# Linear attention with ReLU features: K and V of two groups loaded as one transfer

## The chip, the cores and the metric

The kernel runs on one NeuronCore of one Trainium2 chip. The metric is the device time of one execution in microseconds (us); the time given for a kernel is the median of its runs.

## The reference

Q, K and V have the shape 8 x 12 x 512 x 64 in float32, so there are 96 heads of 512 rows by 64 columns.

```python
Q_feat = np.maximum(0, Q)
K_feat = np.maximum(0, K)
KV = np.einsum('bhkd,bhkv->bhdv', K_feat, V)
K_sum = np.sum(K_feat, axis=2)
numerator = np.einsum('bhqd,bhdv->bhqv', Q_feat, KV)
denominator = np.einsum('bhqd,bhd->bhq', Q_feat, K_sum)
return numerator / (denominator[:, :, :, None] + 1e-10)
```

For each head a 64 x 64 matrix KV and a vector K_sum of 64 are made from K and V; each row of Q is then multiplied by them and divided. There is no softmax, so K and V of a head must be complete before any of its output can be made.

## The kernel before

The 96 heads are worked in 12 octets of 8 heads (numbered 0 to 11), and an octet's K and V in 2 groups of 4 heads. Octet o holds the groups 2o and 2o + 1. A group's K is a tile `k_sb` of 128 partitions; a partition holds 16 rows of one head, which lie in HBM as one run of 16 x 64 x 4 bytes = 4 KB. V is the same in `v_sb`. Q of an octet is one tile `q_sb`, 128 partitions with 32 rows each, 8 KB in HBM. Output of an octet leaves from `o_sb`, 128 partitions with 8 KB each.

The loads are issued from POOL (GpSimd, `nc.gpsimd.dma_start`) and change float32 to bfloat16 on their way, so the 4 KB of a row arrive as 2 KB. The K and V of octet 0 are the exception: they come as float32 over the SP and ACT queues (L109, L110, `k_first` and `v_first`). For each later octet, `load_octet` issues five transfers in this order: K and V of the first group, K and V of the second group (`load_kv`, L97 and L99), then Q (`load_q`, L103). Octets 1 to 5 are issued ahead of all work. Octet o + 6 is issued in `store` (L279), just behind the store of octet o (L289), which POOL issues too. POOL issues in program order, so a store whose `o_sb` is not ready holds up the loads behind it. The stores of the last two octets go over SP (L284, L287) and the last one is cut into two halves.

The transfers of POOL share eight completion semaphores in turn: a transfer is issued only when the one eight before it has landed. The tile framework puts that wait there. It doesn't stand in the code, and it shows in the profile as POOL waiting for a `k_sb`, `v_sb`, `q_sb` or `out_dram` transfer.

The order of the compute work is written out by hand (`manual_schedule`), one instruction stream per engine. In iteration o of the main loop (L326) and up to o = 8:

- `kvs(o)`: TensorE multiplies K by V for both groups of octet o (L189) into `ps_kv`, and ACT moves the result to `kvd` (L199);
- `prep(2o+2)`, `prep_v(2o+2)`: VectorE (DVE) and ACT make masked copies of K and V of the next octet's first group (L175, L177, L182);
- `backs(o-1)`: TensorE transposes octet o - 1 back (L267), DVE divides into `o_sb` (L273), and the store is issued;
- `denom(o)`, `out_t(o)`: the denominators (L249, L252, L257, L261) and the numerators (L240, L242);
- `prep(2o+3)`, `prep_v(2o+3)`: the second group (L175, L177, L184);
- `qt(o+1)`: Q of the next octet is transposed (L210) and passed through the ReLU (L218).

The later iterations and the part behind the loop do the same in another order, so that the last stores come early. The buffers for `k_sb` and `v_sb` hold 12 groups each.

Of the kernel before, what the change touches and what calls it, by code (L numbers as in the profile page):

```python
# [10 lines left out]
def kernel(  # L11
# [7 lines left out]
    nc = tc.nc  # L19
    B, H, S, D = Q.shape  # L20
    assert D == 64
    P = 128
# [4 lines left out]
    R = S * 4 // P  # L27
# [4 lines left out]
    NO = NG // 2  # L32
    assert NO * 8 == NH and R == 16 and RQ == 32
    DELAY = 5

    fp32 = mybir.dt.float32
    bf16 = mybir.dt.bfloat16
# [3 lines left out]
    def pool(name, bufs, **kw):  # L41
        return ctx.enter_context(tc.tile_pool(name=name, bufs=bufs, **kw))

    consts = pool("consts", 1)
    qin = pool("qin", 7)
    kin = pool("kin", 12)
    vin = pool("vin", 12)
    kfp = pool("kfp", 4)
    rcp = pool("rcp", 2)
    outp = pool("outp", DELAY + 2)  # L50
# [6 lines left out]
    def view(X, f):  # L57
        return X.rearrange("b h s d -> (b h s d)").rearrange("(n p f) -> n p f", p=P, f=f)

    Qr, Kr, Vr, Or = view(Q, RQ * D), view(K, R * D), view(V, R * D), view(out, RQ * D)  # L60
# [31 lines left out]

    q_sb, k_sb, v_sb = {}, {}, {}

    def load_kv(g):
        k_sb[g] = kin.tile([P, R, D], bf16, name="k_sb")
        nc.gpsimd.dma_start(out=k_sb[g].rearrange("p r d -> p (r d)"), in_=Kr[g], single_packet=True)  # L97
        v_sb[g] = vin.tile([P, R, D], bf16, name="v_sb")
        nc.gpsimd.dma_start(out=v_sb[g].rearrange("p r d -> p (r d)"), in_=Vr[g], single_packet=True)  # L99

    def load_q(o):
        q_sb[o] = qin.tile([P, U, 2 * D], bf16, name="q_sb")
        nc.gpsimd.dma_start(out=q_sb[o].rearrange("p u f -> p (u f)"), in_=Qr[o], single_packet=True)  # L103
# [8 lines left out]
    make_identity(nc, ident)  # L112

    def load_octet(o):
        load_kv(2 * o)
        load_kv(2 * o + 1)
        load_q(o)

    for o in range(1, DELAY + 1):
        load_octet(o)  # L120
# [158 lines left out]
    def store(o, o_sb):  # L279
        Ov = Or[o].rearrange("p (r d) -> p r d", d=D)  # L280
        if o == NO - 1:
            for j in range(2):
                rs = slice(RQ // 2 * j, RQ // 2 * (j + 1))
                nc.sync.dma_start(out=Ov[:, rs], in_=o_sb[:, rs])  # L284
            return
        if o >= NO - 2:
            nc.sync.dma_start(out=Ov, in_=o_sb)  # L287
            return
        nc.gpsimd.dma_start(out=Ov, in_=o_sb, single_packet=True)  # L289
        if o + DELAY + 1 < NO:  # L290
            load_octet(o + DELAY + 1)
# [51 lines left out]
    o = NO - 2  # L343
    g = 2 * NO - 2
# [52 lines left out]
```

## Time and profile before

| What | Value |
|---|---|
| median of 3 runs | 127.1 us (126.67 to 127.52) |
| the profiled execution | 126.42 us |
| its span, first to last instruction | 124.7 us |
| instructions | 2642 |
| TensorE, VectorE, ScalarE, GpSimd busy | 69%, 67%, 65%, 31% of the span |
| mean busy share of the DMA engines | 90% or more in 38 of 40 slices |
| HBM read and written | 37.75 MB and 12.58 MB |
| transfers issued by POOL | 66: 22 of K, 22 of V, 12 of Q, 10 stores |
| transfers issued by SP and ACT | 5 |

Busy shares are means over the span. The span is what the profile shows of an execution; 1.7 us of the execution lie around it. A "DMA packet" in the profile is one row of a transfer, or one of the 16 packets of 4 bytes (one for each DMA engine) that end a transfer. The megabytes under the queues count what arrives, so a row of K counts 2 KB there though 4 KB of HBM were read.

### The profile page before, as it was taken

To read this page: it belongs to the slowest core of one execution; us is meant where nothing else is said; L and a number is where in the kernel's file an instruction comes from. 1 tells how busy PE (TensorE), PEld (TensorE's weight loads), DVE (VectorE), ACT (ScalarE), POOL (GpSimd) and SP (SyncE) were. 2 spreads that over 40 slices of the span, in tenths; PEclk is the share of its full clock that TensorE was granted. 3 is DMA by queue.
4 is the path that set the end of the run, shared out by engine and by line. 5 is a ranking of instruction groups with operands and counts; after the bars stand their busy time and mean duration, and the time that the engine had idled before them with its cause. 6 is when DMAs were issued, how large, how long until landed. Compare 5 with 4: busy or idle time off the path is not lost.

```text
span 124.7 us, 2642 instructions
## 1 busy us (share of the span) xinstructions
PE 86.4 (69%) x1067; PEld 77.5 (62%) x1067; DVE 83.1 (67%) x192; ACT 80.8 (65%) x112; POOL 38.1 (31%) x72
## 2 busy tenths in 40 slices
PE   0005794688989979897883799793696598697700
PEld 0005573687878879784872798692685497695500
DVE  2719804979899797979569346929739608979430
ACT  0008958969899898989886428976489266537100
POOL 6902624405245241233253144243333220100000
PEclk9999999999999999999999559999999859999997
DMA  3999999999999999999999999999999999999992
GB/s 95 397 310 205 216 205 210 215 206 215 206 214 210 210 216 358 229 216 333 257 213 291 299 210 256 335 210 234 354 220 217 352 233 218 323 426 415 429 410 121
DMA packets 10236, 32.67 MB, mean 262 GB/s; under 512 B 1136, under 2 KB 1136, under 8 KB 8560
## 3 DMA queue, kind: packets, MB, share of 16 engines
q0 software_dynamic: 9504, 28.32, 94.9%
q1 hardware_dynamic: 576, 3.15, 6.3%
q10 hardware_dynamic: 144, 1.05, 2.1%
q8 instruction: 8, 0.13, 0.4%
q14 instruction: 4, 0.03, 0.1%
HBM read 37.75 MB, written 12.58 MB: 404 GB/s over the span
## 4 chain that ended last, share of the span: by engine, by line
DVE 34%; DMA 27%; PE 24%; ACT 6%; issue 4%; DVEq 1%; ACTq 0%
DVE o_sb L273 15%; DMA q_sb<-in_Q_dram 11%; DMA v_sb<-in_V_dram 9%; PE ps_kv L189 8%; PE ps_bk L267 7%; DMA v_first<-in_V_dram 7%; DVE kf L175 5%; PE ps_kv L165 5%; DVE vo_all L177 3%; PE ps_qt L210 3%; DVE vo_all L184 3%; DVE den L257 2%; DVE rec L261 2%; DVE own L252 2%; ACT vo_all L158 2%
## 5 line engine op out<-in xcount | busy, mean ns | idle before, releaser
L273 DVE TENSOR_TENSOR o_sb<-ps_bk,rec 128x1024 f32<-128x1024 f32 x24 | 28.3, 1218 | 14.6 <-PE ps_bk L267 14.6
L189 PE MATMUL ps_kv<-vo_all,kf 128*128 128x132 bf16 x352 | 26.3, 234 | 6.6 <-DVE vo_all L184 6.1
L189 PEld LDWEIGHTS <-kf 128*128 128x128 bf16 x352 | 23.8, 104 | 7.9 <-issue 4.2
L242 ACT COPY ot_sb<-ps_ot 128x1024 f32<-128x1024 f32 x24 | 24.1, 1012 | 5.3 <-PE ps_ot L240 4.4
L199 ACT CAST kvd<-ps_kv 64x260 bf16<-64x260 f32 (+1 forms) x46 | 16.5, 360 | 15.2 <-PE ps_kv L189 14.1
L210 PE MATMUL ps_qt<-ident,q_sb 128*128 128x128 bf16 x192 | 15.2, 242 | 13.6 <-DMA q_sb<-in_Q_dram 13.6
L218 ACT ACTIVATE qt<-ps_qt 128x1024 bf16<-128x1024 bf16 x23 | 22.4, 1024 | 2.3 <-PE ps_qt L210 2.2
L267 PE MATMUL ps_bk<-ident,ot_sb 128*128 128x128 f32 x192 | 23.4, 276 | 0.4 <-ACT ot_sb L242 0.4
L175 DVE TENSOR_SCALAR kf<-k_sb,mask 128x1024 bf16<-128x1024 bf16 x44 | 18.3, 458 | 7.6 <-DMA k_sb<-in_K_dram 7.5
L210 PEld LDWEIGHTS <-q_sb 128*128 128x128 bf16 x192 | 13.6, 110 | 14.5 <-DMA q_sb<-in_Q_dram 14.4
L267 PEld LDWEIGHTS ps_bk<-ident,ot_sb 128*128 128x128 f32 x192 | 21.3, 144 | 0.7 <-ACT ot_sb L242 0.7
L97 POOL DMA_DIRECT2D k_sb<-in_K_dram x22 | 13.2, 602 | 25.3 <-DMA q_sb<-in_Q_dram 21.1
L240 PE MATMUL ps_ot<-qt,kvd 128*128 128x256 bf16 x96 | 14.0, 271 | 8.0 <-DVE o_sb L273 7.2
L99 POOL DMA_DIRECT2D v_sb<-in_V_dram x22 | 12.1, 551 | 20.3 <-ACT qt L218 6.4
L240 PEld LDWEIGHTS <-kvd 128*128 128x128 bf16 x96 | 9.0, 97 | 10.9 <-issue 9.0
L182 ACT ACTIVATE vo_all<-v_sb,mask 128x1024 bf16<-128x1024 bf16 x10 | 11.5, 1153 | 0.6 <-DMA v_sb<-in_V_dram 0.4
L177 DVE TENSOR_SCALAR vo_all<-v_sb,mask 128x1024 bf16<-128x1024 bf16 x22 | 10.6, 482 | 1.1 <-DMA v_sb<-in_V_dram 1.1
L289 POOL DMA_DIRECT2D out_dram<-o_sb x10 | 5.4, 544 | 13.7 <-DVE o_sb L273 4.8
L103 POOL DMA_DIRECT2D q_sb<-in_Q_dram x12 | 6.8, 570 | 8.9 <-DMA k_sb<-in_K_dram 2.7
L249 PEld LDWEIGHTS <-qt 128*128 128x128 bf16 x192 | 6.8, 96 | 3.8 <-issue 1.8
L249 PE MATMUL ps_den<-kvd,qt 128*128 128x16 bf16 x192 | 7.2, 180 | 2.3 <-ACT kvd L169 1.7
L158 ACT ACT_TABLE_LOAD x1 | 1.3, 1283 | 9.8 <-DMA v_first<-in_V_dram 9.8
(33 smaller groups left out, 50.6 us busy)
## 6 DMA issues: line engine op xcount, KB each, us to landing
out_dram<-o_sb POOLq DMA_DIRECT2D x10, 1024.0 KB, 14.3
q_sb<-in_Q_dram POOLq DMA_DIRECT2D x12, 512.0 KB, 13.1
k_sb<-in_K_dram POOLq DMA_DIRECT2D x22, 256.0 KB, 12.1
v_sb<-in_V_dram POOLq DMA_DIRECT2D x22, 256.0 KB, 12.1
v_first<-in_V_dram ACTq DMA_DIRECT2D x1, 1024.0 KB, 9.0
k_first<-in_K_dram SPq DMA_DIRECT2D x1, 1024.0 KB, 8.8
out_dram<-o_sb SPq DMA_DIRECT2D x1, 1024.0 KB, 7.0
out_dram<-o_sb SPq DMA_DIRECT2D x2, 512.0 KB, 4.2
```

Of the source, the lines that this page charges most:

```text
L97: nc.gpsimd.dma_start(out=k_sb[g].rearrange("p r d -> p (r d)"), in_=Kr[g], single_packet=True)
L175: nc.vector.tensor_scalar(kf[g][:, :, s, :], k_sb[g], scalar1=0.0, scalar2=mask[:, 0, s:s + 1], op0=Alu.max, op1=Alu.mult)
L177: nc.vector.tensor_scalar(vo[g % NB][:, :, 0, 2:D + 2], v_sb[g], scalar1=mask[:, 1, 0:1], scalar2=None, op0=Alu.mult)
L189: nc.tensor.matmul(ps_kv[:, g % 2, 0:2 * (D + 2)].rearrange("p (t d) -> p t d", t=2), kf[g][:, r, :, :].rearrange("p s d -> p (s d)"), vo[ ...
L199: copy(kvd[o % NK][64 * c:64 * c + 64, 4 * gs.start + s:4 * gs.stop:2, c * D1:c * D1 + D1].rearrange("p (g t) d -> p g t d", t=2), ps_kv[6 ...
L210: nc.tensor.transpose(ps[:, u, :], q_sb[o][:, i * (U // 2) + u, :], ident)
L218: nc.scalar.activation(to, ps, Act.Relu)
L240: nc.tensor.matmul(ps[:, i], kvd[o % NK][:, h, 1:2 * D + 1], q[:, :, h, :], start=True, stop=True, skip_group_check=True)
L242: nc.scalar.copy(ot[o][:, :, 4 * j:4 * j + 4], ps.rearrange("p h u c -> p u h c"))
L249: nc.tensor.matmul(ps[:, u], qt_sb[o % NZ][:, u, :], kvd[o % NK][:, :, 0:2 * D1:2 * D1 - 1], start=True, stop=True, skip_group_check=True)
L267: nc.tensor.transpose(ps[:, 2 * v:2 * v + 2].rearrange("p c d -> p (c d)"), ot[o][:, 8 * j + v].rearrange("p h c -> p (h c)"), ident32)
L273: nc.vector.tensor_tensor(o_sb[:, rs], ps, rec[o][:, rs].unsqueeze(2).to_broadcast([P, 16, D]), op=Alu.mult)
```

## The change

For octets 1 to 8 (`PAIRS` is 9), K of both groups is loaded by one transfer of 2 x 128 rows of 4 KB into one tile with room for two groups, and V by another. The order in the queue becomes K of both groups, V of both groups, Q. Octets 9 to 11 still load their groups one by one, in the order K, V, K, V, Q, but into the halves of such double tiles. The tiles `k_sb` and `v_sb` come from pools with 6 double buffers, which hold 12 groups as before. What the compute engines do, and in which order, is not changed.

```diff
-    kin = pool("kin", 12)
-    vin = pool("vin", 12)
+    kin = pool("kin", DELAY + 1)
+    vin = pool("vin", DELAY + 1)
...
-    def load_kv(g):
-        k_sb[g] = kin.tile([P, R, D], bf16, name="k_sb")
-        nc.gpsimd.dma_start(out=k_sb[g].rearrange("p r d -> p (r d)"), in_=Kr[g], single_packet=True)
-        v_sb[g] = vin.tile([P, R, D], bf16, name="v_sb")
-        nc.gpsimd.dma_start(out=v_sb[g].rearrange("p r d -> p (r d)"), in_=Vr[g], single_packet=True)
+    PAIRS = NO - 3
+
+    def load_kv(o, X, pool_, sb, name):
+        t = pool_.tile([P, 2, R, D], bf16, name=name)
+        for i in range(2):
+            sb[2 * o + i] = t[:, i]
+        if o < PAIRS:
+            nc.gpsimd.dma_start(out=t.rearrange("p n r d -> p n (r d)"),
+                                in_=X[2 * o:2 * o + 2].rearrange("n p f -> p n f"), single_packet=True)
+
+    def load_half(o, i, X, sb):
+        nc.gpsimd.dma_start(out=sb[2 * o + i].rearrange("p r d -> p (r d)"), in_=X[2 * o + i], single_packet=True)
...
     def load_octet(o):
-        load_kv(2 * o)
-        load_kv(2 * o + 1)
+        load_kv(o, Kr, kin, k_sb, "k_sb")
+        load_kv(o, Vr, vin, v_sb, "v_sb")
+        if o >= PAIRS:
+            for i in range(2):
+                load_half(o, i, Kr, k_sb)
+                load_half(o, i, Vr, v_sb)
         load_q(o)
```

## The prediction

> **What bounds the kernel.** I read the page's engine and DMA parts first.
>
> ```profile
> PE 86.4 (69%) x1067; PEld 77.5 (62%) x1067; DVE 83.1 (67%) x192; ACT 80.8 (65%) x112; POOL 38.1 (31%) x72
> ...
> DMA  3999999999999999999999999999999999999992
> ...
> DMA packets 10236, 32.67 MB, mean 262 GB/s; under 512 B 1136, under 2 KB 1136, under 8 KB 8560
> ...
> q0 software_dynamic: 9504, 28.32, 94.9%
> ...
> HBM read 37.75 MB, written 12.58 MB: 404 GB/s over the span
> ```
>
> No compute engine is over 69%, while the DMA engines are busy from the second slice to the last but one. The third and fourth lines give the make-up of the queue: 9504 packets in 66 transfers are 144 each, 128 rows and 16 closing packets of 4 bytes (71 transfers in all x 16 = 1136, the packets under 512 B). Each of the 16 engines thus moves 8 rows and one closing packet of every transfer.
>
> Next, POOL in the timeline, which shows how fast the queue drains, since each issue here ends a wait for the landing of the transfer issued eight before it (columns: start, duration, engine, line, operation; in brackets the idle time before).
>
> ```profile
> 29.69 0.53 POOL L103 DMA_DIRECT2D q_sb<-in_Q_dram  x1 [0.77 <-DMA v_sb<-in_V_dram]
> 30.93 0.53 POOL L97 DMA_DIRECT2D k_sb<-in_K_dram  x1 [0.71 <-DMA k_sb<-in_K_dram]
> 32.16 0.53 POOL L99 DMA_DIRECT2D v_sb<-in_V_dram  x1 [0.70 <-DMA v_sb<-in_V_dram]
> 34.62 0.53 POOL L97 DMA_DIRECT2D k_sb<-in_K_dram  x1 [1.93 <-DMA q_sb<-in_Q_dram]
> ```
>
> Two transfers of K or V, of 0.52 MB, land 1.24 and 1.23 us apart, and a Q of 1.05 MB takes 2.46 us. Twice 1.235 is 2.47, so one large transfer costs nearly what two small ones do. The trace's packet records are finer. On one engine the closing packets stand 1253 ns apart for K and V, 2458 for Q and 2464 for a store, to the nanosecond, over long stretches. Rows of K start every 154 ns. 8 x 154 = 1232, so the rest of a transfer, its closing packet, is about 21 ns; the record of that packet lasts 22 ns.
>
> Last, the chain that ended last and VectorE (DVE) around the octets where the new transfers end.
>
> ```profile
> 72.66 11.46 DMA v_sb<-in_V_dram
> ```
> ```profile
> 72.97 0.88 DVE L175 TENSOR_SCALAR kf<-k_sb,mask 128x1024 bf16<-128x1024 bf16 x2 [3.26 <-DMA k_sb<-in_K_dram]
> 74.30 0.49 DVE L177 TENSOR_SCALAR vo_all<-v_sb,mask 128x1024 bf16<-128x1024 bf16 x1 [0.45 <-DMA v_sb<-in_V_dram]
> 75.88 2.36 DVE L273 TENSOR_TENSOR o_sb<-ps_bk,rec 128x1024 f32<-128x1024 f32 x2 [1.09 <-PE ps_bk L267]
> ...
> 82.93 0.88 DVE L175 TENSOR_SCALAR kf<-k_sb,mask 128x1024 bf16<-128x1024 bf16 x2 [2.04 <-DMA k_sb<-in_K_dram]
> 84.14 0.49 DVE L177 TENSOR_SCALAR vo_all<-v_sb,mask 128x1024 bf16<-128x1024 bf16 x1 [0.33 <-DMA v_sb<-in_V_dram]
> ```
> ```profile
> 114.23 0.34 SPq L287 DMA_DIRECT2D out_dram<-o_sb  x1
> 118.36 1.46 SPq L284 DMA_DIRECT2D out_dram<-o_sb  x2
> ```
>
> The chain waits for V of group 18 (octet 9) until 84.12 and is compute from there to the last stores. But those stores don't set the end alone. The packet records show 15 to 21 packets under way at nearly every microsecond from 4 to 121. The last closing packets of the last store come from 121.8 on the first engine to 123.4 on the slowest, which has worked without a pause. The time is what the slowest DMA engine has to do. The last half-store is issued at 119.49, would need 0.83 us to start (as the first half, 118.36 to its first packet at 119.19), and the slowest engine reaches it only at 123.41 - 1.26 = 122.15: it could come 122.15 - 120.32 = 1.8 us later at no cost.
>
> **The change, part by part.**
>
> Bytes and rows stay: 16 x 16 = 256 rows per engine go into the 16 new transfers.
>
> Closing packets: 32 transfers become 16. 16 x 21 ns = 0.34 us less on every engine, the slowest too, and on the path, since that engine never pauses. The POOL rows above bound it: 2 x 1.235 - 2.46 = 0.01 us per pair, 0.16 in all; the record's own 22 ns gives 0.35. I take 0.35, and the 0.16 stays in the range. On this the Trainium skill ("DMA: Bandwidth & Descriptors", the section "Anatomy of one DMA — SWDGE (gpsimd) path") says that the write of the semaphore is a bubble of about one cycle. By that sentence the saving would be nil and the sum the time before; the 21 ns between the last row and the next transfer disagree with it here.
>
> Row cost in a double transfer: each engine now steps between two places 512 KB apart, 4 KB at each. No transfer before does that. Nearest rows: half of an 8 KB row of Q is (2458 - 21) / 16 = 152 ns; a 4 KB row of the last half-stores starts 156 ns after the one before; and a K row's record lasts 173 ns though the next starts after 154, so 173 is the price if rows no longer overlapped. Over 256 rows these ends are -0.4, +0.5 and +4.9 us. I take 154 and so 0, because read size, written size and row are those of the K rows, and keep both ends.
>
> Issue on POOL: 16 instructions fewer, at 0.55 to 0.60 us each about 9 us less. A double one could take from 0.53 (a Q issue of twice the bytes) to 2 x 0.60 = 1.2 us. Neither counts: POOL idles 0.7 to 1.9 us before each issue above, behind seven transfers still in flight. Without that cover 0.6 us x 16 = 10 us would be exposed. At the start, where eight issues follow each other from 1.26 to 6.2 us, the queue has Q of octet 0 to move until 10.4, so nothing runs dry.
>
> Eight in flight: an octet and its store are now four transfers of 1 MB instead of six. Eight of them last 8 x 2.46 = 19.7 us instead of 13.2, so stores are issued some 6 us earlier against their landing. The loads queued behind a store on POOL wait for its `o_sb`; the outputs of octets 0 to 3 are ready some octets before, and later the queue merely holds less. The order in the queue, hence each landing, stays. No cost. Pool space is the same 12 groups, whose readers finish octets earlier.
>
> Order K, K, V, V: K of the first group lands with the second, 1.25 us later, V 2 x 1.25 = 2.5 us later. Until octet 5 compute runs behind the loads: a period of 7.1 us in the chain (the `own` at 29.80, 36.89 and 43.99) against 3 x 2.46 = 7.4 us of loads, with the loads some 13 us ahead. By my reckoning V of octet 5 lands at 47.3 and is wanted at 47.4. From octet 6 the loads lead, 9.9 us an octet. Then DVE stalls with L273, L252 and the rest of the iteration queued behind its L177. Worst placed is octet 8: L177 moves from 74.30 to 76.8. Behind it come 0.48 + 2.36 + 1.2 (L252, L257, L261) + 1.6 (L175, L177, L184) to 82.4, 1.1 of TensorE at L189 and 1.6 of ACT at L199 to 85.1. In the trace of before ACT's copy L182 for group 18 ran from 84.20 to 85.35 and its next, L242, waited until 86.50. So the copy ends at 86.3 and nearly all the delay is swallowed; about 0.2 us is left, against 1.8 us of slack at the last store. No cost.
>
> Halves in octets 9 to 11: same transfers, same rows, nothing.
>
> Sum: 126.42 - 0.35 = 126.07 us for the profiled execution. The median of the runs, 127.1, is 0.7 above that execution, so the forecast is 127.1 - 0.35 = **126.8 us**. A measurement of this kernel can tell about 1% (1.3 us) from no change, so this would read as no change.
>
> **Rivals.**
>
> Dearer rows (slower). The two places 512 KB apart cost each row overlap. It decides from (1.27 + 0.35) us / 256 = 6.3 ns a row, 160 instead of 154. At 164, halfway to 173, it is 126.8 + 2.6 = 129.4; at 173, 131.7. For it: no row of before shows such stepping. Against it: K, V, Q and stores all run at the same 150 to 156 ns per 4 KB, whatever their direction and place. The Trainium skill ("DMA: Bandwidth & Descriptors", "Latency and other measured facts") reports 207 instead of 214 GB/s for rows at a pitch of 512 KiB. No run here shows it; 3.4% of 154 ns would be 5.2 ns a row, 256 x 5.2 = 1.3 us, and a time of 128.1.
>
> Late V (slower or same). If nothing swallows the 2.5 us and TensorE meets a granted clock of a half there too, as the page shows for two stretches (L189 1.80 instead of 1.11 us, L210 1.71 instead of 0.89), 1.5 us comes on top: 4.0 - 1.8 of slack = 2.2 late, 129.0. For it: DVE waits for K and V at just this place. Against it: the reckoning above, and 9.9 - 7.1 = 2.8 us free in each octet.
>
> Evener engines (faster). If the engines ended together at 122.4 instead of 121.8 to 123.4, and rows cost 152 ns: 126.8 - 1.0 - 0.4 = 125.4. For it: the spread is there. Against it: every transfer gives each engine the same share, and pairing doesn't alter that.
>
> Small ones: the double transfer is carried out as two (127.1), or the second half of a tile is made to wait for the first in octets 9 to 11. Q of octet 0 needs 4.2 us from its issue (1.26) to its first packet (5.43), so three dry spells of up to 4.2 - 1.25 us give 135. Against this, the two halves of the last store already go out separately.
>
> **How the numbers follow.** Forecast 0.51 (126.3 to 127.3 by itself), dearer rows 0.22, late V 0.12, evener engines 0.09, done as two 0.03, waiting halves 0.03. Slower by over 1%: 0.17 of dearer rows, 0.06 of late V, the 0.03, and 0.02 of the forecast's spread, 0.28. Faster by over 1%: 0.08 of evener engines and 0.02, 0.10. The rest, 0.62, within 1%. Range: 125.6, with half of the evener engines, to 129.8, past both middle prices.
>
> **What would show it.** Right: 50 transfers on the POOL queue; closing packets 2 x 1253 - 21 = 2485 ns apart for double ones; DMA busy in every slice but the ends; the end 0.35 us earlier. Wrong: rows over 160 ns apart, a dip in the DMA row at octets 9 to 11, or the last SP stores issued more than 1.8 us later.

## The result and the profile after

The changed kernel takes 126.2 us (5 runs, 125.96 to 126.35) beside 126.89 us of the kernel before (5 runs, 126.67 to 127.52): ratio 0.9933, 95% interval 0.9904 to 0.9962, so 0.5 to 1.2 us less. A second set of runs (e8 below) gave 0.9962, interval 0.9941 to 0.9984. Both lie within 1%. The forecast was 126.8 us, from a base of 127.1 us that two more runs brought to 126.89. The profiled execution went from 126.42 to 126.20 us and its span from 124.65 to 124.42. Among the runs below, only the three longest of e12 fell in a slower state, and its ratio leaves them out.

The page of the changed kernel, parts 1 to 3:

```profile
PE 84.5 (68%) x1067; PEld 75.2 (60%) x1067; DVE 83.2 (67%) x192; ACT 80.5 (65%) x112; POOL 32.4 (26%) x56
...
DMA  2999999999999999999999999999999999999992
...
DMA packets 9980, 32.67 MB, mean 263 GB/s; under 512 B 880, under 2 KB 880, under 8 KB 8304
...
q0 software_dynamic: 9248, 28.31, 94.8%
```

The small packets went from 1136 to 880, 256 = 16 x 16 fewer, and the queue has 16 x 272 + 34 x 144 = 9248 packets. The DMA engines are as busy as before, and of the others only POOL moves by more than 2 points of share, from 31% to 26%.

POOL in the timeline, with the double transfers (L102) and the time to landing from part 6:

```profile
13.65 0.85 POOL L110 DMA_DIRECT2D q_sb<-in_Q_dram  x1 [1.75 <-DMA k_sb<-in_K_dram]
16.11 0.70 POOL L102 DMA_DIRECT2D k_sb<-in_K_dram  x1 [1.61 <-DMA v_sb<-in_V_dram]
18.56 0.71 POOL L102 DMA_DIRECT2D v_sb<-in_V_dram  x1 [1.76 <-DMA q_sb<-in_Q_dram]
```
```profile
k_sb<-in_K_dram POOLq DMA_DIRECT2D x8, 512.0 KB, 19.5
...
k_sb<-in_K_dram POOLq DMA_DIRECT2D x6, 256.0 KB, 13.4
```

A double transfer lands every 2.46 us or so, and eight in flight now last 19.5 us. In the packet records the closing packets of double transfers stand 2486 ns apart (twice 1253 would be 2506), and a row's record still lasts 173 ns. From the closing packet of the first Q to that of the last it is 97.86 us on the slowest engine, where it was 98.19: 0.33 us less. As a mean over the 16 engines it is 97.19 instead of 97.50 us.

VectorE around octet 8, and the last stores:

```profile
73.83 0.88 DVE L186 TENSOR_SCALAR kf<-k_sb,mask 128x1024 bf16<-128x1024 bf16 x2 [2.02 <-DMA k_sb<-in_K_dram]
76.28 0.49 DVE L188 TENSOR_SCALAR vo_all<-v_sb,mask 128x1024 bf16<-128x1024 bf16 x1 [1.56 <-DMA v_sb<-in_V_dram]
76.68 2.35 DVE L284 TENSOR_TENSOR o_sb<-ps_bk,rec 128x1024 f32<-128x1024 f32 x2
...
83.71 0.49 DVE L188 TENSOR_SCALAR vo_all<-v_sb,mask 128x1024 bf16<-128x1024 bf16 x1 [0.33 <-DMA v_sb<-in_V_dram]
```
```profile
112.57 0.34 SPq L298 DMA_DIRECT2D out_dram<-o_sb  x1
116.69 1.46 SPq L295 DMA_DIRECT2D out_dram<-o_sb  x2
```

The copy of V that ran at 74.30 now waits until 76.28, yet V of octet 9 is used at 83.71 (84.14 before) and the last two half-stores are issued 1.67 us earlier than before. The span is only 0.23 us shorter: it doesn't follow those stores.

### The profile page after: what moved, and what is told of

It is laid out like the page before. It is cut to its first block, busy times and chain, and to the rows that moved or that the text cites. A ratio compares the mean times of both kernels' runs of the same rounds, so it can differ in the third digit from the quotient of the medians.

```text
span 124.4 us, 2626 instructions
## 1 busy us (share of the span) xinstructions
PE 84.5 (68%) x1067; PEld 75.2 (60%) x1067; DVE 83.2 (67%) x192; ACT 80.5 (65%) x112; POOL 32.4 (26%) x56
## 3 DMA queue, kind: packets, MB, share of 16 engines
q0 software_dynamic: 9248, 28.31, 94.8%
## 4 chain that ended last, share of the span: by engine, by line
DMA 58%; DVE 17%; PE 13%; issue 2%; POOL 1%; ACT 1%; DVEq 1%; POOLq 0%
DMA v_sb<-in_V_dram 41%; DMA k_sb<-in_K_dram 17%; DVE o_sb L284 9%; PE ps_kv L200 5%; PE ps_bk L278 4%; PE ps_qt L221 3%; DVE kf L186 2%; PE ps_ot L251 1%; DVE vo_all L188 1%; DVE vo_all L195 1%; DVEq L403 1%; ACT ot_sb L253 1%; DVE den L268 1%; DVE rec L272 1%; DVE qt L227 1%
## 5 line engine op out<-in xcount | busy, mean ns | idle before, releaser
L284 DVE TENSOR_TENSOR o_sb<-ps_bk,rec 128x1024 f32<-128x1024 f32 x24 | 28.3, 1218 | 11.4 <-PE ps_bk L278 11.4
L200 PE MATMUL ps_kv<-vo_all,kf 128*128 128x132 bf16 x352 | 24.1, 222 | 6.8 <-DVE vo_all L195 6.3
L200 PEld LDWEIGHTS <-kf 128*128 128x128 bf16 x352 | 21.6, 98 | 8.2 <-issue 4.6
L251 PE MATMUL ps_ot<-qt,kvd 128*128 128x256 bf16 x96 | 15.5, 294 | 10.0 <-DVE o_sb L284 9.1
L278 PEld LDWEIGHTS ps_bk<-ident,ot_sb 128*128 128x128 f32 x192 | 20.8, 141 | 0.7 <-ACT ot_sb L253 0.7
L251 PEld LDWEIGHTS <-kvd 128*128 128x128 bf16 x96 | 9.5, 103 | 13.5 <-issue 11.2
L188 DVE TENSOR_SCALAR vo_all<-v_sb,mask 128x1024 bf16<-128x1024 bf16 x22 | 10.6, 482 | 5.0 <-DMA v_sb<-in_V_dram 5.0
L110 POOL DMA_DIRECT2D q_sb<-in_Q_dram x12 | 7.4, 618 | 15.1 <-DMA k_sb<-in_K_dram 7.2
L300 POOL DMA_DIRECT2D out_dram<-o_sb x10 | 6.1, 605 | 17.9 <-DVE vo_all L195 6.2
L102 POOL DMA_DIRECT2D v_sb<-in_V_dram x8 | 5.8, 726 | 14.6 <-DMA q_sb<-in_Q_dram 8.9
L102 POOL DMA_DIRECT2D k_sb<-in_K_dram x8 | 5.8, 722 | 7.5 <-DMA v_sb<-in_V_dram 3.3
## 6 DMA issues: line engine op xcount, KB each, us to landing
k_sb<-in_K_dram POOLq DMA_DIRECT2D x8, 512.0 KB, 19.5
```

Source lines behind the costliest of these rows:

```text
L102: nc.gpsimd.dma_start(out=t.rearrange("p n r d -> p n (r d)"), in_=X[2 * o:2 * o + 2].rearrange("n p f -> p n f"), single_packet=True)
L188: nc.vector.tensor_scalar(vo[g % NB][:, :, 0, 2:D + 2], v_sb[g], scalar1=mask[:, 1, 0:1], scalar2=None, op0=Alu.mult)
L200: nc.tensor.matmul(ps_kv[:, g % 2, 0:2 * (D + 2)].rearrange("p (t d) -> p t d", t=2), kf[g][:, r, :, :].rearrange("p s d -> p (s d)"), vo[ ...
L251: nc.tensor.matmul(ps[:, i], kvd[o % NK][:, h, 1:2 * D + 1], q[:, :, h, :], start=True, stop=True, skip_group_check=True)
L278: nc.tensor.transpose(ps[:, 2 * v:2 * v + 2].rearrange("p c d -> p (c d)"), ot[o][:, 8 * j + v].rearrange("p h c -> p (h c)"), ident32)
L284: nc.vector.tensor_tensor(o_sb[:, rs], ps, rec[o][:, rs].unsqueeze(2).to_broadcast([P, 16, D]), op=Alu.mult)
```

## The experiments

Theory 1: each transfer left out saves its closing packet, 21 ns on every DMA engine, and the time is what the slowest engine has to move. Theory 2: the last SP stores, freed by a shifted clock, also pay. Theory 3: more bytes in flight pay. Every ratio is to the kernel before in the same set of runs.

**e1, the order without the pairs.** For octets 1 to 8 the double transfer becomes two:

```diff
-            nc.gpsimd.dma_start(out=t.rearrange(...), in_=X[2 * o:2 * o + 2].rearrange(...), single_packet=True)
+            for i in range(2):
+                load_half(o, i, X, sb)
```

> Undoes the pairing and keeps the rest: octets 1 to 8 are loaded in the order K, K, V, V into the double tiles, but as single transfers of 128 rows, 66 in all. Theory 1 (closing packets: each transfer left out saves about 21 ns on every DMA engine, and nothing else changed): as before, ratio 1.000, closing packets of K and V 1253 ns apart. Theory 2 (the later V moves the compute, TensorE keeps its clock in the last octets, and the last stores over SP come earlier): the part of the gain beyond 0.35 us stays, ratio 0.997, and the last SP store is issued before 118.4 us. Theory 3 (more bytes in flight under eight transfers keep the engines better fed): as before, 1.000, for the bytes in flight are those of before.

Measured: 1.0005 (0.9985 to 1.0025). Its last stores in the timeline:

```profile
112.56 0.34 SPq L298 DMA_DIRECT2D out_dram<-o_sb  x1
116.69 1.46 SPq L295 DMA_DIRECT2D out_dram<-o_sb  x2
```

They are as early as in the changed kernel, and the span is 124.7 us as before. Early last stores pay nothing: theory 2 falls here. The gain is in the pairs.

**e2 and e3, half of the pairs.** The condition `o < PAIRS` becomes `o <= 4` in e2 and `5 <= o <= 8` in e3; other octets load singles.

> Pairs only in octets 1 to 4, singles from 5 on: 8 transfers fewer than before. Theory 1: 8 x 21 ns = 0.17 us less, ratio 0.9987. Theory 2: from octet 5 on all lands in the old order, so the last stores come as before and only the 0.17 us are saved, 0.9987. Theory 3: the queue is deep only before 45 us, where compute is not waiting for loads: 0.9987 at best.

> Pairs only in octets 5 to 8: 8 transfers fewer than before. Theory 1: 0.17 us less, ratio 0.9987, the same as with pairs in octets 1 to 4. Theory 2: the late V of octets 6 to 8 is there, so the last stores are early and most of the gain of the change is here, 0.17 + 0.35 us, 0.996. Theory 3: the same sign as theory 2, 0.996, but with the last SP stores issued as late as before.

Measured: e2 0.9976 (0.9953 to 0.9998), e3 0.9984 (0.9962 to 1.0005). The two halves can't be told apart, and both intervals hold theory 1's 0.9987. The last stores of e2, then of e3:

```profile
116.75 1.46 SPq L294 DMA_DIRECT2D out_dram<-o_sb  x2
```
```profile
118.07 1.46 SPq L294 DMA_DIRECT2D out_dram<-o_sb  x2
```

Theory 2 had them the other way round, early in e3. The span is 124.4 us in e3 against 124.6 in e2: again the later stores don't make the later end.

**e4 and e9, more pairs.** `PAIRS = NO` in e4 and `PAIRS = NO - 1` in e9; NO is the number of octets, 12.

> Pairs in all octets 1 to 11: 22 transfers fewer than before, 6 fewer than in the changed kernel. Theory 1: 22 x 21 ns = 0.46 us less than before, 0.13 less than the changed kernel, unless the last stores come too late. The last V is 2.5 us later for the first group of octet 11, and the changed kernel issues its last store about 3.2 us before the slowest engine wants it (117.8 + 0.83 against 123.16 - 1.26), so it should just be covered: ratio 0.9925 to 0.994 if the changed kernel is at 0.9933. If the cover is not enough, V lands 2.5 us later than now and the time is up to 1 us over the changed kernel: 1.000.

> Pairs in octets 1 to 10, singles in octet 11 only: 4 transfers fewer than the changed kernel. Theory 1: 4 x 21 ns = 0.08 us less than the changed kernel, ratio 0.0007 below it, too little to be told, as long as the last store is still issued before about 121 us; the later V of octet 10 may take the last stores up to 2 us later, as pairs in all octets did (120.39 against 116.69).

Measured: e4 0.9965 (0.9946 to 0.9985), e9 0.9990 (0.9967 to 1.0014); the changed kernel is at 0.9962 in the set of e9. Neither beats it. From the kernel before, theory 1 alone gives e4 0.9963 (22 x 21 ns). e4's profiled execution took 126.99 us with a span of 125.2, and is the longest of its 12 runs (median 126.08); it shows a price that can come with the last octets paired. SP in its timeline:

```profile
120.39 1.46 SPq L295 DMA_DIRECT2D out_dram<-o_sb  x2
```

and its DMA share from 116 to 120 us beside that of the changed kernel (start and end; span; busy time of PE, PEld, DVE, ACT, POOL; clock; DMA share; GB/s), e4 first:

```profile
116.00:120.00 4.00, 3.42 (x34) 2.71 (x30) 2.29 (x5) 1.89 (x2) 0.00 (x0) 1.00 0.86 358
```
```profile
116.00:120.00 4.00, 0.28 (x3) 0.04 (x1) 1.79 (x2) 0.00 (x0) 0.00 (x0) 0.87 1.00 421
```

In this execution the DMA engines wait for the last stores. All 16 end between 123.80 and 123.96 us there, while in the changed kernel they end between 121.4 and 123.2, each when its own work is done. In e9 the last stores were late as well:

```profile
118.77 1.46 SPq L295 DMA_DIRECT2D out_dram<-o_sb  x2
```

That is 2.08 us later than in the changed kernel, at the same span of 124.4 us.

The packet records of these runs, and of three more below, tell the price of a transfer more finely than the times do. From the closing packet of the first Q to that of the last, as a mean over the 16 DMA engines, it is:

| transfers fewer than before | kernels | us |
|---|---|---|
| 0 | before, e1 | 97.50, 97.47 |
| 8 | e2, e3 | 97.37, 97.34 |
| 16 | changed, e8, e11, e12 | 97.19, 97.20, 97.24, 97.19 |
| 20 | e9 | 97.12 |
| 22 | e4 | 97.05 |

A straight line through the ten values falls by 19 ns for each transfer left out, and no value lies more than 0.05 us off it. So the saving goes with the number of transfers, whichever octets they are in, at about the price of theory 1. The slowest engine alone tells less: it needs 97.86 us in the changed kernel and 98.09 in e8, which is the same kernel.

**e5 and e6, last stores without their compute.** In both kernels `store` of octet 9 also issues the SP stores of octets 10 and 11, from the same tile; the other two calls issue nothing. The output of octets 10 and 11 is left out.

```diff
+        if o == NO - 3:
+            nc.sync.dma_start(out=Or[NO - 2]..., in_=o_sb)
+            for j in range(2):
+                nc.sync.dma_start(out=Or[NO - 1]...[:, rs], in_=o_sb[:, rs])
```

> The kernel before, but the stores of octets 10 and 11 send the finished tile of octet 9 and so wait for no compute of the last two octets (the output of octets 10 and 11 is left out; all compute is still done). What is left is the DMA work. Theory 1: the last stores had 1.8 us of slack in the profiled execution, so the time stays at that of the best executions of before, 126.4 to 126.9, ratio 0.997 to 1.000. Theory 2: the executions of before that are slower than its profiled one are so because the last stores came late; they lose that, ratio 0.996 to 0.997. Theory 3: as before, 1.000.

> The changed kernel with the same edit (stores of octets 10 and 11 send the tile of octet 9, whose output is left out). Theory 1: 0.35 us under the kernel before with this edit, with the same spread. Theory 2: as the changed kernel itself, 0.993, and 0.35 us under the edited kernel before; the distance of the two edited kernels is smaller than that of the two unedited ones. Theory 3: 0.993, and the distance stays 0.7 us.

Measured: e5 1.0212 (1.0172 to 1.0252), e6 1.0138 (1.0105 to 1.0171). All three theories missed e5, which none of them had above 1.000. The early SP stores now run beside the stores of POOL, and the last transfer to end is POOL's: in e5 SP's last packet ends at 121.14 us and POOL's at 123.38, where it was 123.42 and 119.39. e5 by windows:

```profile
120.00:124.00 4.00, 0.00 (x0) 0.00 (x0) 0.00 (x0) 0.00 (x0) 0.00 (x0) 0.50 0.62 261
124.00:128.00 4.00, 0.00 (x0) 0.00 (x0) 0.00 (x0) 0.00 (x0) 0.00 (x0) 0.50 0.00 0
```

Nothing moves after 124, and the span is 127.2. The packet records say the same: the last packet ends at 123.38 in e5 and at 123.42 in the kernel before; 123.29 in e6 and 123.17 in the changed one. So the DMA work itself is not shorter when the last stores wait for nothing, which is theory 1's claim. The pair was meant to give the distance of the two edited kernels. It is 0.0074, or 0.9 us, where theory 1 said 0.35; 0.66 us of it lie behind the last packet (3.86 us in e5, 3.20 in e6), so it decides nothing.

**e7 and e10, more closing packets.** Q as two transfers of 128 rows of 4 KB, in all octets (e7) or in octets 1 to 11 (e10):

```diff
-        nc.gpsimd.dma_start(out=q_sb[o]..., in_=Qr[o], single_packet=True)
+        n = 2 if o else 1    # e7: n = 2
+        for i in range(n):
+            cs = slice(RQ * D // n * i, RQ * D // n * (i + 1))
+            nc.gpsimd.dma_start(out=q_sb[o]...[:, cs], in_=Qr[o][:, cs], single_packet=True)
```

> The changed kernel with Q of each octet loaded as two transfers of 128 rows of 4 KB instead of one of 8 KB: 12 closing packets more, and the rows of Q at 154 ns per 4 KB instead of 152.3. Theory 1: per octet 16 x 154 + 2 x 21 = 2506 instead of 2458 ns, 48 ns x 12 = 0.58 us more than the changed kernel, ratio 0.993 + 0.0046 = 0.998. Theory 2: the same, as the last stores have 3 us of slack in the changed kernel. Theory 3: more, for the queue is also less deep (7 MB instead of 8 MB in flight).

> The changed kernel with Q of octets 1 to 11 as two transfers of 128 rows of 4 KB; Q of octet 0, which runs beside the two other queues, stays whole. Theory 1: 11 x (2506 - 2458) ns = 0.53 us more than the changed kernel, ratio 0.0042 above it. If it is again 1.2 us or more above the changed kernel, the closing packets and row prices do not account for it.

Measured: e7 1.0073 (1.0049 to 1.0096), e10 1.0037 (1.0010 to 1.0063). The direction is right and the size is not: e10 is 0.0075, or 0.95 us, above the changed kernel of its set, where 0.53 was reckoned. The rate is as reckoned, with halves of Q 1253 ns apart. The rest shows as one gap. e10's data rate by slices of 3.1 us:

```profile
GB/s 84 392 320 208 211 190 210 212 210 212 210 212 208 211 213 366 225 214 324 261 212 289 301 203 241 349 211 223 366 209 208 365 224 210 332 413 431 431 405 102
```

The sixth slice has 190 where its neighbours have 210, which is 20 / 210 x 3.1 = 0.30 us. In the packet records the first half of Q of octet 1 closes 1575 ns (the middle engine) after the V before it instead of 1253, on all engines alike. In e7 the same place has no gap, but the first Q, which runs beside the two other queues, closes at 10.63 us on the middle engine instead of 10.11. What makes these two losses is open; each comes at one place and not per transfer. In e10 POOL needed 1.54 us for the issue at 13.51 us, where such an issue takes about 0.72 elsewhere; whether that belongs to the gap is not shown.

**e8, the changed kernel again.**

> The changed kernel, unaltered, beside the next three on one chip. Theory 1 (16 closing packets of 21 ns less on each DMA engine): 0.35 us under before, ratio 0.9973; with the runs of pairs in a half of the octets at 0.9976 and 0.9984 the sum of the two gives 0.9960. Theory 4 (something beside the closing packets): 0.9933 again, 0.85 us.

Measured: 0.9962 (0.9941 to 0.9984), 126.3 against 126.65 us. The interval holds theory 1's 0.9973. 0.9933 lies just outside it, and the interval of the first set ends at 0.9962, which leaves 0.9973 out. The larger gain of the first set did not come again; what made it is open.

**e11, fewer bytes in flight.** `pool("kin", 3)` and `pool("vin", 3)`, that is 3 double buffers instead of 6.

> The changed kernel with 3 double buffers for K and 3 for V instead of 6, so that a load has to wait until the octet three before it has been prepared, and fewer bytes are in flight. Theory 1: as long as the queue never runs dry the time is that of the changed kernel, within 0.1%. Theory 3 (the deeper queue is what pays): back at the time of before or above, 1.000 or more.

Measured: 0.9966 (0.9943 to 0.9990). Its time to landing, and below it that of the kernel before:

```profile
k_sb<-in_K_dram POOLq DMA_DIRECT2D x8, 512.0 KB, 15.6
```
```profile
k_sb<-in_K_dram POOLq DMA_DIRECT2D x22, 256.0 KB, 12.1
```

It is 15.6 us instead of 19.5, and the gain is the same, where theory 3 wanted it gone: theory 3 falls. The queue of e11 is still deeper than that of the kernel before, so this alone would not rule out a small part; the table above, where the saving goes with the number of transfers alone, leaves little room for one.

**e12, later last stores.**

```diff
     idle(6, o + 1)
+    for i in range(4):
+        nc.vector.memset(fill, 0.0)
     backs(o + 1)
```

> The changed kernel with four memsets of 128 x 1120 float32 on VectorE (about 1.06 us each, by the 492 ns of the 128 x 520 ones) ahead of the last octet's division. In the changed kernel VectorE is free from 113.8 to 115.4 there, so the last stores are issued about 2.6 us later, near 119.3 and 120.4. Theory 1: the slowest DMA engine wants the last half-store only at 121.9, it needs 0.83 us to start, so 3.25 us are free and the time stays, within 0.2%. Theory 2 (the last stores set the end): 2.6 us more, ratio 0.997 + 0.020.

Measured: 1.0008 (0.9976 to 1.0039), but its runs spread from 126.25 to 128.78. Four of the ten (126.25 to 126.66) are as short as runs of the kernel before. I read the profiled execution of 128.01 us instead. The delay was mis-sized. VectorE and SP in its timeline, and the window from 120 to 122 us:

```profile
116.74 0.99 DVE L381 MEMSET fill<- 128x1120 f32 x1 [0.30 <-DVE fill L381]
...
120.23 2.29 DVE L285 TENSOR_TENSOR o_sb<-ps_bk,rec 128x1024 f32<-128x1024 f32 x2
```
```profile
121.42 1.46 SPq L296 DMA_DIRECT2D out_dram<-o_sb  x2
```
```profile
120.00:122.00 2.00, 0.00 (x0) 0.00 (x0) 2.00 (x3) 0.00 (x0) 0.00 (x0) 0.95 0.05 20
```

Each memset waits 0.30 us for the one before, and they began at 115.45 and not 113.8 (the store of octet 10, ahead of them, was 1.46 us later too), so the stores moved by 4.7 us (116.69 to 121.42), past the 3.25 us of cover. The DMA engines then stand idle, at a share of 0.05. By the 0.83 us to start, the second half-store, issued near 122.55, starts at 123.38, 1.5 us after 121.9; the span is 1.8 us longer (126.2). That is near the slack as reckoned, from the far side. That 2.6 us cost nothing was not measured here; e3's stores, 1.4 us later than the changed kernel's, and e9's, 2.1 us later, both at the same span, are the nearer evidence.

## Why the prediction was right, point by point

- The number: 126.2 us lies in the stated range of 125.6 to 129.8, but under the 126.3 to 127.3 that the forecast gave itself. Of the 0.6 us between 126.8 and 126.2, 0.2 is the base of 127.1, and for the rest the first set gained more than the 0.35 us of the term. That the range held it so easily is owed to its width, which is there for the rivals.
- Bound: right. The last packet ends within 0.2 us of the same place whether the last stores wait for compute or not (e5, e6) and whether they go out at 116.7 or 118.4 (e1 and before).
- Closing packets: the term was 0.35 us; the packet records show 2486 ns for a double transfer where 2485 was said, and 16 x 19 ns = 0.30 us as a mean over the engines; the 0.33 on the slowest engine came out so near in part by luck, since that of e8 gives 0.10. The first set of runs gave more, 0.85 us (0.5 to 1.2), the second 0.48 (0.2 to 0.75). In the four later sets the kernel before had medians of 126.41, 126.41, 126.65 and 126.79 us, all under the 126.89 of its first five runs, so a part of the 0.85 may be those five; that is not shown. On the Trainium skill's sentence ("DMA: Bandwidth & Descriptors", "Anatomy of one DMA — SWDGE (gpsimd) path") that the write of the semaphore is a bubble of about one cycle: by it nothing would have been gained, and e1 (1.0005) beside e8 (0.9962) and the 19 ns a transfer show that the number of transfers pays.
- Rows 512 KB apart: 154 ns, so 16 x 154 + 21 = 2485. The rival of dearer rows did not occur. The Trainium skill's figure for a pitch of 512 KiB ("DMA: Bandwidth & Descriptors", "Latency and other measured facts") is for copies from the sync and scalar queues; it does not carry over to two such places in turn with 4 KB at each, as the 154 ns show.
- Issue on POOL: 0.72 us for a double one, inside 0.53 to 1.2, and hidden.
- Late V: L188 at 76.28 where 76.8 was reckoned, and swallowed as said by the time L284 starts, 84.47 against 84.54. The 0.2 us left over for the last stores was wrong in sign: they came 1.67 us earlier. TensorE's granted clock was 1.00 from 100 to 104 us, where it had been 0.70; the prediction had thought of the clock only as a loss. That the clock moved the stores is not shown. It made no difference, since the engines had work until 123.2 either way.
- Evener engines: not seen. They still end 1.8 us apart, 121.4 to 123.2, where it was 1.6.
- The halves in octets 9 to 11 go out one by one, 1.25 us apart at the closing packets; no waiting.

## What to carry to other kernels

In this kernel, where the DMA engines never pause, the price of the edit could be counted on them: so many rows and so many closing packets, by the spacing in the packet records. Merging 16 pairs of transfers took 16 x 19 ns off each engine, and neither earlier last stores (e1) nor the deeper queue (e11) was seen to add to it. Take the mean over the engines and several executions: the slowest engine moved by 0.2 us between two executions of one kernel. Pairing the last octets too brought no more (e4, e9), and in the execution of e4 that was profiled, the longest of its runs, the last stores came out 3.7 us later and the engines stood waiting.

## What the runs showed of the hardware that I had not expected

- The two kernels whose last transfer is POOL's end later behind it. In e5 the last landing is at 123.73 us and the span 127.2; in the kernel before, where SP's store lands last at 123.74, the span is 124.65. In e6 it is 123.61 and 126.5. The runs don't show what the time is spent on, nor that nothing else in these two kernels makes it.
- TensorE's granted clock fell at other places with no change in its program: 0.53 from 68 to 72 and 0.70 from 100 to 104 us before, 0.61 and 1.00 after, with 0.75 from 76 to 80. Two executions of the changed kernel differ as well: e8 has 0.50 from 68 to 72 and 1.00 from 76 to 80. So two traces don't show that the change did it.
- The 16 engines drift apart in lumps: in the changed kernel the slowest falls back by 1.0 us at the Q of octet 2 and keeps about that distance for 50 us. At that time (25.08 us) the trace has one packet of 16 KB of the instruction queue, of 0.98 us. That this packet is what holds the engine up is not shown, since the records don't name the engine.
